# One decoder step: the stage between attention and the mLSTM state (output projection, norm, xm tiles, gates) put into one stated order

## The chip, the cores and the metric

The kernel runs on one core of one Trainium2 chip. A core has five engines with queues of their own: TensorE (PE, matrix products), VectorE (DVE), ScalarE (ACT), GpSimd (POOL) and SyncE (SP, which here issues most DMA transfers). Each engine takes its instructions in order; where one needs what another engine or a transfer makes, it waits on a semaphore, and everything behind it in the queue waits too. The metric is the device time of one execution in microseconds, as the median of several runs.

## What is computed

One inference step of a two-layer decoder with d_model 1024, for a prompt of 512 new tokens and 8 sample sequences with one new token each, so 520 token columns. Layer 0 is native sparse attention, layer 1 an mLSTM with four heads of width 512. All data are float32. The stage in question covers the end of layer 0 and the front of layer 1:

```python
x = x + out0 @ w_out0                      # layer 0: output projection and residual
h = rmsnorm(x, norm_w[1])
proj = h @ w_in                            # layer 1, 1024 -> 4096: xm and z
xm, z = proj[..., :D_INNER], proj[..., D_INNER:]
xpad = jnp.concatenate([conv_buf, xm], axis=1)
conv = conv_b
for j in range(CONV_W):                    # CONV_W = 4
    conv = conv + xpad[:, j:j + T] * conv_w[j]
c = jax.nn.silu(conv)
q = jnp.einsum('btnj,nji->btni', cb, w_qkv[0])     # blocks of 4 columns; cb = c, xb = xm in blocks
k = jnp.einsum('btnj,nji->btni', cb, w_qkv[1])
v = jnp.einsum('btnj,nji->btni', xb, w_qkv[2])
gpre = jnp.concatenate([q, k, v], axis=-1) @ w_gate + b_gate
ig, fl = gpre[..., :M_HEADS], jax.nn.log_sigmoid(gpre[..., M_HEADS:])
# then the mLSTM cell with states C, n, m; out = (hn * norm_w + skip * c) * silu(z); out @ w_out
```

## The kernel before

The activations lie transposed, features on the 128 partitions and the 520 tokens along the row, in two column halves of 260; the sample columns are the last 8 of half 1. A float32 product is made of three products of a reduced type: value and weight are each split into a high half (hi, a copy that rounds) and a low half (lo, the rest), and `mm3` issues hi x hi, lo x hi and hi x lo. In the trace a high or low half of a weight is called whi or wlo, of the normed input hhi or hlo, of the attention's result uo.

Weights come tile by tile (1024 x 128). `load_w` issues the transfer of the raw tile (wraw, 512 KB) on SP, the cast to whi on ACT, and the subtraction that gives wlo on DVE or POOL, by a table with a letter for each tile (LO_O for the output projection, LO_XM for xm). There are two buffers each of wraw, whi and wlo, so that a tile's parts overwrite those of the tile before the last.

The stage has these parts, in the order of the program:

- Output projection: a loop over 8 row tiles ft and the two halves c. For each, PE makes 24 matmuls into a PSUM buffer (mm), DVE adds the result to x1 (the residual stream, loaded from in_xT, called x in the trace), and `split_x` makes hhi on ACT and hlo on DVE. `rms_acc` squares x (ACT, sq) and adds it to a running sum sacc (DVE); `rms_close` sums it over the partitions with one PE product (s<-sacc) and makes the factor rr.
- `prepare`, spread between these: the gate weights folded with the block-diagonal q, k and v weights into FG (three wg products on POOL, three reduces ft on DVE), and the conv state's rows scv.
- xm loop over 16 tiles of layer 1's first projection: `xm_proj` for both halves (24 matmuls and one DVE eviction each), the next tile's `load_w`, three block-diagonal weights bd (POOL), `xm_tile` (causal conv, cva: one ACT and four DVE instructions), `xm_silu` (three on ACT, cvs, and the product CT on DVE), `xm_val` for the tile before (four matmuls t<-bd,xm and four copies to VT), `xm_gate` for the tile before that (products d for the sample columns, and, for each pair of tiles, eight matmuls s<-CT,FG and s<-xm,FG that add into the gate sums).
- Tail: the first z tile (`zm_tile(0)`), gates of tiles 14 and 15, `gate_samples` (a chain of some 15 small instructions on DVE and ACT from the sample columns of the gate sums, ss, to the decays sr, with two small PE products t<-ss and t<-sr), and the values of tile 15.

Then comes the state stage, where 64 state tiles cs of 512 KB are loaded, scaled, updated and stored.

What sets the order: the attention stage ahead and the state stage behind are recorded as pieces (one engine call, or one chain of matmuls into one buffer) and replayed in an order written as a table of numbers; all five engines then keep that order. Between the two, the order is of three kinds. In the output projection SP keeps the written order and the tile scheduler places the others. In the xm loop PE, ACT and DVE keep the written order; SP and POOL are placed. In the tail all are placed, with hints (`issue_after`). Every engine call goes through one helper, `Engine.call`, so that all instructions have its line, L407 before; groups are told apart by tile names.

Of the kernel before, what the change touches and what calls it, by code (L numbers as in the profile page):

```python
# [9 lines left out]
F32 = mybir.dt.float32  # L10
# [220 lines left out]
)  # L231
KSC = float(np.float32(512.0 ** -0.5))
# [97 lines left out]
class Pool:  # L330

    def __init__(self, rec, pool, bufs):
        self.rec, self.pool, self.bufs = rec, pool, bufs
# [7 lines left out]
class Rec:  # L341
# [8 lines left out]
    def cut(self):  # L350
        self.open = None

# [90 lines left out]
def step_kernel(ctx, tc, ap):  # L443
# [1054 lines left out]
    dctx.close()  # L1498
    r1 = ctx.enter_context(ExitStack())
# [16 lines left out]
    for k in range(4):  # L1516
        S.dma_start(x1[:, 2 * k:2 * k + 2], ap["xT"][:, 2 * k:2 * k + 2])
    def prepare():

        par0 = xp_.tile([128, 16, 7], F32, name="par0")  # L1520
        SP.dma_start(par0, ap["m_par"])
        wc0 = xp_.tile([128, 3, 16, 4], F32, name="wc0")
# [22 lines left out]
    for ft, c in [(ft, c) for ft in range(8) for c in range(2)]:  # L1545
        if ft not in wo:
            wo[ft] = load_w(ap["w_o"][ft], 8, eng=E[LO_O[ft]])
        if ft == 4 and c == 0:
            next(prep)
        w = wo[ft]  # L1550
# [4 lines left out]
        add = V.tensor_add(x1[:, ft, cs], x1[:, ft, cs], po[:, :CH])  # L1555
        if (ft, c) == (6, 0):
            with tc.issue_after(add.ins):
                next(prep, None)
        split_x(c, ft, x1[:, ft, cs], 1)
        if c:  # L1560
            S.dma_start(x1d[:, ft], x1[:, ft])
        rms_acc(sacc[c], ft == 0, x1[:, ft, cs], xn)
        if ft == 7:
            rms_close(c, sacc[c], xn)
    wx0 = load_w(ap["m_in"][0], 8, eng=E[LO_XM[0]])
    l0.close()
    xctx.close()
# [3 lines left out]
    l1 = ctx.enter_context(ExitStack())  # L1571
    cv = pool_of(l1, name="cv", bufs=1)
# [7 lines left out]
    l1s = pool_of(l1, name="l1s", bufs=1)  # L1580
# [32 lines left out]
    se = pool_of(l1, name="st0", bufs=1)  # L1613
# [18 lines left out]
    mctx = l1.enter_context(ExitStack())  # L1632
    mi = pool_of(mctx, name="mi", bufs=2)
    m1 = pool_of(mctx, name="mi1", bufs=1)
# [12 lines left out]
    def xm_proj(ft, c):  # L1647
# [5 lines left out]
        return V.tensor_mul(xm[:, c * CH:(c + 1) * CH], po[:, :CH], rr[c])  # L1653
# [3 lines left out]
    def xm_tile(ft):  # L1657
# [3 lines left out]
        S.activation(a, xm, AF.Identity, scale=par[:, ft, 3:4], bias=par[:, ft, 4:5])  # L1661
        for d in (1, 2, 3):
            V.scalar_tensor_tensor(a[:, d:512], xm[:, 0:512 - d], par[:, ft, 3 - d:4 - d], a[:, d:512],
# [4 lines left out]
    def xm_silu(ft):  # L1668
# [4 lines left out]
        G.tensor_scalar(CS[:, ft], ct[:, 512:520], par[:, ft, 6:7], None, op0=OP.mult)  # L1673
# [57 lines left out]
    def gates_of(gs, gi, gf, src):  # L1731
        V.tensor_copy(gs, src)
        for k, (nm, dst) in enumerate((("sel_i", gi), ("sel_f", gf))):
            po = xb()[:, :gs.shape[-1]]
# [3 lines left out]
    def gate_samples():  # L1738
        ss = m1.tile([128, 8, 8], F32, name="ss")
        gs, gi, gf, e, y, m0, m = (ss[:, k] for k in range(7))  # L1740
        gates_of(gs, gi, gf, pgt[1][:, CH - 8:CH])
# [15 lines left out]
    def gate_rows():  # L1757
        rows = [big(f"rows{i}", n=T) for i in range(3)]
        A_, W_, EM = rows
        gs = big("gs")  # L1760
        gi = big("gi")
        gf = big("gf")
        for c in range(2):
            cs = slice(c * CH, min((c + 1) * CH, T))
            gates_of(gs[:, cs], gi[:, cs], gf[:, cs], pgt[c][:, :min(CH, T - c * CH)])
        e = big("lse")
        y = big("lsy")
        log_sigmoid(*(x[:, :T] for x in (y, gf, e, gs)))

        V.memset(gs[:, 0:512], 1.0)  # L1770
        bcum = gf[:, 0:512]
        V.tensor_tensor_scan(bcum, gs[:, 0:512], y[:, 0:512], 0.0, op0=OP.mult, op1=OP.add)
        a = e[:, 0:512]
        V.tensor_sub(a, gi[:, 0:512], bcum)
        V.tensor_tensor_scan(A_, gs[:, 0:512], a, -HUGE, op0=OP.mult, op1=OP.max)
        m = gs[:, 0:512]
        V.tensor_add(m, bcum, A_)
        SP.dma_start(ap["o_mp"], m[:, 511:512])
        S.activation(EM, m, AF.Exp, scale=-1.0)
# [15 lines left out]
    for ft in range(16):  # L1795
        xst[ft] = [block_diag(mi, wc[:, t, ft], "bd", 12) for t in range(3)]
        xm_proj(ft, 0)
        if ft < 15:
            xm_load(ft + 1)
# [919 lines left out]
```

## Time and profile before

| | us |
|---|---|
| median of 3 runs (lowest, highest) | 1136.6 (1132.46, 1137.16) |
| the profiled execution | 1135.48 |
| its span, first to last instruction | 1132.8 |
| PE busy in the span | 1058.4 (93%) |
| DVE busy | 813.6 (72%) |
| ACT busy | 602.0 (53%) |
| POOL busy | 277.2 (24%) |
| the stage, first projection matmul to first matmul of z tile 1 | 210.74 |

The 2.7 us between span and execution lie outside the recorded instructions. Busy time is the union of an engine's instructions; matmuls overlap in the pipeline, so one takes 0.28 us in the record but the next may start 0.12 us after it. The clock column of a view is the share of full speed that was granted to PE in that stretch.

### The profile page before, as it was taken

Reading aid. Unit: us, or ns where it says so; the run is one execution under the profiler, and the core shown is the slowest. Engines: PE = TensorE matmul, PEld = TensorE weight load, DVE = VectorE, ACT = ScalarE, POOL = GpSimd, SP = SyncE. Lnnn points to the kernel's source line nnn. Section 1 sums busy time; section 2 is a strip of 40 time slices with the busy share of each in tenths; the row PEclk is TensorE's granted clock in tenths of the full one; section 3 lists DMA queues with packets and bytes.
Section 4 is the critical chain, followed back from the end, with each engine's and each line's share of the span. In section 5 each row is a group of like instructions: output and inputs, shape, how many; then the busy total and the mean of one; then the engine's idle time right before and its main releaser. Section 6 shows DMA issues by size and latency. Waiting matters only on the chain.

```text
span 1132.8 us, 24065 instructions
## 1 busy us (share of the span) xinstructions
PE 1058.4 (93%) x8563; PEld 929.7 (82%) x8563; DVE 813.6 (72%) x1988; ACT 602.0 (53%) x1326; POOL 277.2 (24%) x306
## 2 busy tenths in 40 slices
PE   6999999999998999999999998999999999999985
PEld 5999998999977867779888996798856577877885
DVE  7867744786489888857776676775666858878786
ACT  5332434545477766753444453666656746555544
POOL 3024233223201001004522231320222314232111
PEclk9999999999999899999999998999999999999988
DMA  7554643133436313455434451687698787969432
GB/s 231 166 189 132 204 126 117 38 101 119 137 97 208 94 57 118 143 192 163 134 132 135 166 168 65 221 268 277 194 310 304 233 277 236 364 198 317 167 82 88
DMA packets 124929, 197.18 MB, mean 174 GB/s; under 512 B 16253, under 2 KB 66302, under 8 KB 124554
## 3 DMA queue, kind: packets, MB, share of 16 engines
q1 hardware_dynamic: 116602, 181.32, 49.2%
q10 hardware_dynamic: 8208, 14.34, 3.5%
q8 instruction: 67, 1.10, 0.4%
q14 instruction: 52, 0.43, 0.1%
HBM read 145.89 MB, written 58.10 MB: 180 GB/s over the span
## 4 chain that ended last, share of the span: by engine, by line
PE 28%; DMA 10%; DVE 9%; issue 3%; ACT 3%; POOL 1%; SPq 1%; DVEq 0%; ACTq 0%; POOLq 0%
PE mm L407 18%; PE t L407 4%; PE s L407 4%; DMA zd<-zt 4%; DMA wraw<-in_m_in 4%; PE d L407 2%; ACT whi L407 1%; DVE x L407 1%; DMA wraw<-in_m_out 1%; DVE VT L407 1%; DVE sacc L407 1%; DVE zt L407 1%; SPq L407 1%; DVE wlo L407 1%; DVE CT L407 1%
## 5 line engine op out<-in xcount | busy, mean ns | idle before, releaser
L407 PE MATMUL mm<-hhi,whi 128*128 128x260 f32 (+1 forms) x976 | 283.2, 290 | 10.4 <-DVE zt L407 6.7
L407 PE MATMUL mm<-hhi,wlo 128*128 128x260 f32 (+1 forms) x976 | 278.5, 285 | 5.3 <-DVE wlo L407 5.3
L407 PE MATMUL mm<-hlo,whi 128*128 128x260 f32 (+1 forms) x976 | 277.2, 284 | 0.0
L407 PEld LDWEIGHTS mm<-hhi,whi 128*128 128x128 f32 (+1 forms) x976 | 183.9, 188 | 19.6 <-issue 7.7
L407 PEld LDWEIGHTS mm<-hhi,wlo 128*128 128x128 f32 (+1 forms) x976 | 183.9, 188 | 7.0 <-DVE wlo L407 6.7
L407 PEld LDWEIGHTS mm<-hlo,whi 128*128 128x128 f32 (+1 forms) x976 | 183.7, 188 | 0.7
L407 POOL TENSOR_TENSOR wlo<-wraw,whi 128x1024 fp32r<-128x1024 f32 (+1 forms) x52 | 106.6, 2051 | 255.7 <-ACT whi L407 239.0
L407 ACT ACTIVATE whi<-wraw 128x1024 fp32r<-128x1024 f32 (+1 forms) x98 | 88.9, 908 | 115.6 <-PE mm L407 53.2
L407 DVE SCALAR_TENSOR_TENSOR cs<-t,wk,cs 128x512 f32<-128x512 f32 x128 | 88.4, 743 | 14.0 <-PE t L407 9.9
L407 ACT ACTIVATE s<-s,mn 128x512 f32<-128x512 f32 (+3 forms) x128 | 71.3, 559 | 27.3 <-DVE mn L407 25.4
L407 ACT ACTIVATE cs<-cs,SBC 128x1024 f32<-128x1024 f32 x64 | 70.7, 1141 | 15.0 <-PE d L407 15.0
L407 PE MATMUL s<-phi,w1h 128*128 128x256 f32 (+1 forms) x256 | 77.9, 304 | 0.7 <-DVE hs L407 0.5
L407 PE MATMUL s<-plo,w1h 128*128 128x256 f32 (+1 forms) x256 | 74.8, 292 | 2.5 <-DVE plo L407 2.5
L407 DVE TENSOR_TENSOR wlo<-wraw,whi 128x1024 fp32r<-128x1024 f32 (+2 forms) x50 | 54.6, 1093 | 30.7 <-ACT whi L407 30.3
L407 PE MATMUL s<-phi,w1l 128*128 128x256 f32 (+1 forms) x256 | 74.7, 292 | 0.0
L407 PE MATMUL mm<-uh,whi 128*128 128x260 f32 x224 | 66.9, 299 | 2.8 <-ACT sq L407 2.8
L407 DVE CUSTOM_DVE_ANT_0 s<-s,D 128x512 f32<-128x512 f32 (+3 forms) x128 | 59.4, 485 | 9.7 <-PE s L407 8.6
L407 PE MATMUL mm<-uh,wlo 128*128 128x260 f32 x224 | 64.3, 287 | 0.0
L407 PE MATMUL mm<-ul,whi 128*128 128x260 f32 x224 | 64.2, 287 | 0.0
L407 PEld LDWEIGHTS s<-plo,w1h 128*128 128x128 f32 x256 | 49.2, 192 | 3.2 <-POOL wlo L407 2.2
L407 PE MATMUL s<-KA,qst 128*128 128x256 f32 (+3 forms) x128 | 48.5, 385 | 2.3 <-DVE mn L407 1.6
L407 PEld LDWEIGHTS s<-phi,w1h 128*128 128x128 f32 x256 | 49.0, 192 | 1.5 <-PE mm L407 0.7
(425 smaller groups left out, 2605.1 us busy)
## 6 DMA issues: line engine op xcount, KB each, us to landing
cs<-in_state_C SPq DMA_DIRECT2D x64, 512.0 KB, 5.4
o_cs<-cs SPq DMA_DIRECT2D x64, 512.0 KB, 4.9
praw<-in_cache SPq DMA_DIRECT2D x128, 128.0 KB, 2.4
dk<-in_cache SPq DMA_DIRECT2D x128, 128.0 KB, 2.2
wraw<-in_m_in SPq DMA_DIRECT2D x32, 512.0 KB, 4.2
wraw<-in_m_out SPq DMA_DIRECT2D x32, 256.0 KB, 3.8
wraw<-in_w_kv SPq DMA_DIRECT2D x11, 512.0 KB, 4.8
wraw<-in_w_q SPq DMA_DIRECT2D x8, 512.0 KB, 3.3
```

The source lines that it names most:

```text
L407: return f(*[real(x) for x in a], **{n: real(x) for n, x in k.items()})
```

## The change

Everything from the output projection through the values of tile 15 is recorded as well, 712 pieces, and replayed with `R.run(NE, CALLS1, MOVED1)`, with the order of all five engines as in the table CALLS1. MOVED1 lists 97 pieces that go to another engine (`swapped`): eight casts to whi from ACT to DVE (output tiles 3 and 5, xm tiles 0, 1, 5, 7, 8, 9); 28 of the 64 VT copies from DVE to ACT; five CT products and ten of the 14 sacc adds from DVE to POOL; seven wlo from DVE to POOL (output tiles 2, 3, xm tiles 4, 5, 6, 7, 9) and five from POOL to DVE (output tiles 4 to 7, xm tile 0); 25 of the 48 bd products, the three wg and three scv products, one FG sum, wkr and one z product from POOL to DVE. The loads of x1 and the stores of it (x1d) go from ACT's queue to SP's. par0 and wc0 move to a pool that stays open through the xm loop, which reads them in place of par and wc. The pools of layer 0 are closed and those of layer 1 opened by two recorded pieces on SP (`to_layer_1`, `to_xm`) in the middle of the stage. `gate_rows`, which nothing calls, is deleted.

```diff
+CALLS1 = (
+    21, 0, 66, 44, 28, 64, 70, 65, 63, 15, 22, 1, 3, 26, 2, 4, 16, 25, 29, 45, 46, 108, 9, 5, 6, 30, 8, 60, 17,
...
+MOVED1 = (
+    20, 30, 36, 43, 45, 46, 52, 62, 67, 68, 69, 71, 72, 73, 86, 88, 89, 95, 102, 105, 112, 117, 124, 127, 147,
...
     def __init__(self, rec, pool, bufs):
-        self.rec, self.pool, self.bufs = rec, pool, bufs
+        self.rec, self.pool, self.bufs, self.barrier = rec, pool, bufs, None
...
+    def later(self, fn, tiles, pools):
+
+        for p in pools:
+            p.barrier = len(self.pieces)
+        self.fn("SP", 0.0, 0.0, fn, w=tiles)
...
+    R.on = True
+    for k in range(8):
+        uo[k] = R.have(uo[k], [128, 2, NTOK], F32R)
...
     for k in range(4):
-        S.dma_start(x1[:, 2 * k:2 * k + 2], ap["xT"][:, 2 * k:2 * k + 2])
+        SP.dma_start(x1[:, 2 * k:2 * k + 2], ap["xT"][:, 2 * k:2 * k + 2])
+    par0 = pr_.tile([128, 16, 7], F32, name="par0")
+    wc0 = pr_.tile([128, 3, 16, 4], F32, name="wc0")
...
         if c:
-            S.dma_start(x1d[:, ft], x1[:, ft])
+            SP.dma_start(x1d[:, ft], x1[:, ft])
...
+    def to_layer_1():
+        l0.close()
+        ctx.enter_context(l1)
+        cv.pool, l1s.pool = (pool_of(l1, name=n, bufs=1).pool for n in ("cv", "l1s"))
...
+    R.later(to_layer_1, list(uo.values()), (cv, l1s))
+    R.later(to_xm, list(uo.values()) + [xp_, xn], (se, mi, m1))
...
-    order_ = ctx.enter_context(ExitStack())
-    order_.enter_context(tc.manual_schedule(engines={mybir.EngineType.PE, mybir.EngineType.Activation,
-                                                   mybir.EngineType.DVE}))
     for ft in range(16):
-        xst[ft] = [block_diag(mi, wc[:, t, ft], "bd", 12) for t in range(3)]
+        R.at("xmw", ft)
+        xst[ft] = [block_diag(mi, wc0[:, t, ft], "bd", 12) for t in range(3)]
...
         if ft < 13:
-            with tc.issue_after(last["w"]):
-                win_copy(ft)
-                if ft in (3, 6, 9):
-                    win_copy(12 + ft // 3)
+            for n in [ft] + ([12 + ft // 3] if ft in (3, 6, 9) else []):
+                R.fn("SP", 0.4, 1.0, lambda n=n: win_copy(n), r=[xms[ft + 1][0][0]])
...
     xm_silu(15)
-    order_.close()
...
     xm_val(15)
+    with tc.manual_schedule(engines=every):
+        R.run(NE, CALLS1, MOVED1)
     mctx.close()
     pctx.close()
```

In the projection the order of PE's row tiles and halves was (0,0), (0,1), (1,0), (1,1) and so on; now it is (1,1), (1,0), (0,0), (0,1), (3,1), (3,0), (2,0), (2,1), (4,1), (4,0), (5,1), (5,0), (6,0), (6,1), (7,0), (7,1), then the first sum s<-sacc, xm tile 0's half 0, and the second sum.

DVE at the start of the projection. The x rows are adds of a matmul result to x1; sacc and hlo are as above. Before:

```order
L407 TENSOR_TENSOR uo<-us,uo 128x8 x8
L407 TENSOR_TENSOR x_9218<-x_9218,mm 128x260 x3
L407 SCALAR_TENSOR_TENSOR hlo_9195<-x_9218,nw,hhi_9193 128x260
L407 SCALAR_TENSOR_TENSOR hlo_9196<-x_9218,nw,hhi_9194 128x260
L407 SCALAR_TENSOR_TENSOR hlo_9195<-x_9218,nw,hhi_9193 128x260
L407 TENSOR_TENSOR sacc_9223<-sacc_9223,sq 128x260
L407 TENSOR_TENSOR x_9218<-x_9218,mm 128x260
L407 TENSOR_TENSOR wlo<-wraw,whi 128x1024 x2
```

and now:

```order
L461 TENSOR_TENSOR uo<-us,uo 128x8 x8
L461 TENSOR_TENSOR x_9238<-x_9238,mm 128x260 x2
L461 CAST whi<-wraw 128x1024
L461 TENSOR_TENSOR x_9238<-x_9238,mm 128x260 x2
L461 SCALAR_TENSOR_TENSOR hlo_9380<-x_9238,nw,hhi_9345 128x260
L461 TENSOR_TENSOR wg<-wg,wc_9246 128x512
L461 SCALAR_TENSOR_TENSOR hlo_9391<-x_9238,nw,hhi_9383 128x260
```

The cast is that of output tile 3; it stands between the adds of tile 1 and those of tile 0, and its subtraction is now on POOL, while two subtractions that stood on DVE further down are gone.

PE at the end of the stage. d<-CT,bd and d<-xm,bd are a tile's gate products, s<- its gate sums, mm<-hhi the first z tile, t<-ss and t<-sr the two sample products, t<-bd,xm the values of tile 15, t<-cst,VS and t<-gs the start of the state stage. Before:

```order
L407 MATMUL s<-CT_9834,FG 32x260
L407 MATMUL s<-xm_11278,FG 32x260
L407 MATMUL d<-CT_9834,bd 128x8 x2
L407 MATMUL d<-xm_11278,bd 128x8
L407 MATMUL t<-ss,cst 128x8 x2
L407 MATMUL t<-sr,cst 128x24 x4
L407 MATMUL t<-bd,xm_11278 128x128 x4
L407 MATMUL t<-cst,VS 8x128 x4
```

and now (the second half of z tile 0, 24 matmuls, is left out at the dots):

```order
L461 MATMUL t<-ss,cst 128x8 x2
L461 MATMUL d<-CT_11200,bd 128x8 x2
L461 MATMUL d<-xm_11084,bd 128x8
L461 MATMUL s<-CT_11002,FG 32x260
L461 MATMUL s<-xm_10814,FG 32x260
L461 MATMUL s<-CT_11090,FG 32x260
L461 MATMUL s<-xm_10825,FG 32x260
...
L461 MATMUL d<-CT_11090,bd 128x8 x2
L461 MATMUL d<-xm_10825,bd 128x8
L461 MATMUL t<-sr,cst 128x24 x4
L461 MATMUL t<-bd,xm_11298 128x128 x4
```

Between t<-ss and t<-sr, where before stood nothing, now stand the products of tiles 13 and 11, half of a gate sum and half of z tile 0; behind the values of tile 15 come more gate sums, which before stood ahead.

SP where the projection ends. wraw<-in_m_in is the load of an xm tile, o_conv a store of xm tile 0. Before:

```order
L407 DMA stm<-in_state_m 128x8
L407 DMA wraw<-in_m_in 128x1024
L407 DMA o_conv<-xm_9901 128x11
L407 DMA o_vwin<-in_vwin 16x8176
```

with two loads of xm tiles further up, and now:

```order
L461 DMA x1d<-x_9238 128x520
L461 DMA nT<-in_state_n 128x128
L461 DMA par<-in_m_par 128x112
L461 DMA o_vwin<-in_vwin 16x8176
L461 DMA wraw<-in_m_in 128x1024
L461 DMA stm<-in_state_m 128x8
L461 DMA o_conv<-xm_9883 128x11
```

with three further up: the load of the fourth xm tile now stands ahead of the first o_conv store, where before it was the third's.

## Rows read from the trace of the kernel before

**Rows 1.** The busy time of each engine in five stretches that make up the stage: the projection, the xm loop up to its last matmul, the first z tile, the sample gates and values, and the start of the state stage. Columns: stretch, its length, then busy us and instructions of PE, PE's weight loads, DVE, ACT and POOL, the granted clock, the DMA share and GB/s.

```profile
499.70:553.55 53.85, 48.49 (x388) 47.00 (x387) 36.25 (x62) 20.58 (x47) 19.51 (x14) 1.00 0.50 167
553.55:685.84 132.29, 125.95 (x1088) 119.53 (x1086) 94.14 (x218) 58.57 (x83) 40.87 (x67) 1.00 0.42 141
685.84:691.70 5.86, 5.86 (x53) 5.86 (x50) 3.54 (x10) 2.71 (x6) 0.31 (x1) 1.00 0.03 5
691.70:704.60 12.90, 8.13 (x54) 6.25 (x52) 6.85 (x39) 4.00 (x11) 1.34 (x3) 0.77 0.13 32
704.60:710.44 5.84, 5.82 (x23) 1.98 (x24) 3.79 (x16) 2.61 (x4) 0.00 (x0) 0.63 1.02 402
sum 210.74, PE 194.25 PEld 180.62 DVE 144.57 ACT 88.46 POOL 62.02; mean PE 38.85 PEld 36.12 DVE 28.91 ACT 17.69 POOL 12.40
```

**Rows 2.** What PE waited for, from the views of its waits: the first three rows in the projection (499.7 to 553.55), the next two in the xm loop (553.55 to 686), the last two in the tail. Columns: total us, times, longest.

```profile
PE mm L407 <- DVE x L407: 2.6, 3, 1.5
PE s L407 <- DVE sacc L407: 2.0, 1, 2.0
PE mm L407 <- DVE wlo L407: 0.6, 1, 0.6
...
PE mm L407 <- DVE wlo L407: 5.3, 7, 0.9
PE mm L407 <- ACT whi L407: 1.0, 1, 1.0
...
PE t L407 <- DVE sr L407: 3.5, 1, 3.5
...
PE t L407 <- DVE gs L407: 1.3, 1, 1.3
```

**Rows 3.** The view of waits of all engines in the stage, the row of ACT's casts.

```profile
ACT whi L407 <- DMA wraw<-in_m_in: 42.5, 12, 4.8
```

**Rows 4.** The timeline at the start of the stage: a row of PE, then of ACT, DVE and ACT's queue. Columns: start, length, engine and operation, and in brackets the idle time before it and what ended it.

```profile
507.17 0.51 PE L407 MATMUL mm<-uo,whi 128*128 128x260 f32 x2 [1.54 <-DVE x L407]
...
501.01 0.89 ACT L407 ACTIVATE uo<-us 128x8 fp32r<-128x8 f32 x8
...
501.75 0.70 DVE L407 TENSOR_TENSOR uo<-us,uo 128x8 fp32r<-128x8 f32 x8
...
502.60 1.79 ACTq L407 DMA_DIRECT2D x<-in_xT  x4
```

**Rows 5.** The timeline of PE in the tail.

```profile
692.36 0.41 PE L407 MATMUL s<-CT,FG 128*32 128x260 f32 x1
...
693.91 0.61 PE L407 MATMUL d<-CT,bd 128*128 128x8 f32 x4
...
694.60 0.59 PE L407 MATMUL t<-ss,cst 128*128 128x8 f32 x4
698.71 0.62 PE L407 MATMUL t<-sr,cst 128*128 128x24 f32 x2 [3.52 <-DVE sr L407]
```

**Rows 6.** Windows of the tail, PE alone: stretch, length, PE busy and instructions, granted clock, DMA share and GB/s.

```profile
696.00:698.00 2.00, 0.00 (x0) 1.00 0.33 131
698.00:708.00 10.00, 8.02 (x31) 0.53 0.45 150
708.00:710.00 2.00, 2.00 (x14) 0.78 1.05 407
710.00:712.00 2.00, 2.00 (x17) 1.00 0.59 177
```

**Rows 7.** The groups of instructions by form: of DVE and POOL in the stage, and, the two CAST rows, of DVE in the whole span. Columns: names, shapes, count, busy us, mean ns of one, idle time before them.

```profile
L407 DVE TENSOR_TENSOR wlo<-wraw,whi 128x1024 fp32r<-128x1024 f32 x17 | 21.5, 1270 | 22.3 <-ACT whi L407 22.3
L407 DVE SCALAR_TENSOR_TENSOR hlo<-x,nw,hhi 128x260 fp32r<-128x260 f32 x16 | 17.2, 1084 | 6.3 <-ACT hhi L407 6.3
L407 DVE COPY VT<-t 128x128 f32<-128x128 f32 x64 | 14.0, 279 | 1.6 <-PE t L407 1.6
...
L407 DVE TENSOR_TENSOR CT<-cva,cvs 128x520 f32<-128x520 f32 x16 | 11.5, 720 | 3.4 <-ACT cvs L407 3.4
L407 DVE TENSOR_TENSOR sacc<-sacc,sq 128x260 f32<-128x260 f32 x14 | 7.5, 539 | 0.0
...
L407 POOL TENSOR_TENSOR bd<-cst,wc 128x128 f32<-128x128 f32 x48 | 30.4, 662 | 69.9 <-PE d L407 62.7 <-DVE rr L407 7.2
L407 POOL TENSOR_TENSOR wlo<-wraw,whi 128x1024 fp32r<-128x1024 f32 x6 | 14.6, 2429 | 30.2 <-ACT whi L407 30.2
...
L407 DVE CAST phi<-praw 128x1024 fp32r<-128x1024 f32 x20 | 16.5, 835 | 14.3 <-PE s L407 8.4 <-ACT hsg L407 5.3 <-ACT plo L407 0.4
...
L407 DVE CAST whi<-wraw 128x1024 fp32r<-128x1024 f32 x3 | 2.0, 682 | 0.0
```

**Rows 8.** A POOL subtraction and a DVE instruction that overlap, from the timelines of the two, and from the view by tile the shortest, median and longest hlo in ns.

```profile
521.53 2.39 POOL L407 TENSOR_TENSOR wlo<-wraw,whi 128x1024 fp32r<-128x1024 f32 x1 [18.01 <-ACT whi L407]
521.89 2.32 DVE L407 SCALAR_TENSOR_TENSOR hlo<-x,nw,hhi 128x260 fp32r<-128x260 f32 x1 [1.00 <-ACT hhi L407]
...
L407 DVE SCALAR_TENSOR_TENSOR hlo<-x,nw,hhi x16: 483/489/2579, 510.7 to 555.5; 128x260 fp32r<-128x260 f32 x16
```

**Rows 9.** The windows view, columns as in rows 1, of two stretches with a stated order: projections in the attention layer, and the start of the state stage.

```profile
40.00:120.00 80.00, 79.52 (x619) 78.97 (x619) 56.65 (x95) 28.15 (x82) 21.76 (x18) 0.98 0.56 175
720.00:740.00 20.00, 18.03 (x134) 15.88 (x133) 16.73 (x25) 13.13 (x23) 6.43 (x7) 0.91 0.55 191
```

More of the change, by code (lines that the diff above doesn't have):

```diff
@@ L351, in cut, with have @@
         self.open = None
+    def have(self, tile, shape, dtype):
+        b = Base(None, shape, dtype, {})
+        b.t = tile
+        return Lazy(b)
+    def later(self, fn, tiles, pools):
+        for p in pools:
+            p.barrier = len(self.pieces)
+        self.fn("SP", 0.0, 0.0, fn, w=tiles)
     def add(self, eng, m, a, k):
@@ L1498, in step_kernel @@
     dctx.close()
+    R.on = True
+    for k in range(8):
+        uo[k] = R.have(uo[k], [128, 2, NTOK], F32R)
+    for k in wo:
+        wo[k] = [R.have(t, [128, 8, 128], F32R) for t in wo[k]]
     r1 = ctx.enter_context(ExitStack())
@@ L1755, in gate_samples @@
         V.tensor_copy(SBC.rearrange("p h a b -> p (h a b)"), po[:, 0:96])
[L1757 to L1779, printed above, removed]
-        V.tensor_scalar(EM, EM, XMAX, None, op0=OP.min)
-        na = se.tile([128, 1], F32, name="na")
-        V.tensor_scalar(na, A_[:, 511:512], -1.0, None, op0=OP.mult)
-        S.activation(W_, a, AF.Exp, bias=na)
-        V.tensor_scalar(W_, W_, KSC, None, op0=OP.mult)
-        po = xb()
-        for i in range(4):
-            PE.transpose(po[:, i * 128:(i + 1) * 128], a[:, i * 128:(i + 1) * 128], ident)
-        V.tensor_copy(aT, po.rearrange("p (i h r) -> p i h r", i=4, h=4)[:, :, :, 0])
-        for i in range(3):
-            SP.dma_start(rd[:, i], rows[i][0:128:32])
@@ L1807, in step_kernel @@
             xm_silu(ft - 1)
-        late = xm_proj(ft, 1)
+        R.at("xm", ft, 1)
+        xm_proj(ft, 1)
         if ft > 1:
+            R.at("gate", ft - 2)
             xm_gate(ft - 2)
+        R.at("conv", ft)
         conv[ft] = xm_tile(ft)
+        R.at("misc")
         if ft == 8:
@@ L1817, in step_kernel @@
             c_load(ft + ECS - 16)
+    R.at("silu", 15)
     xm_silu(15)
-    order_.close()
-    G.tensor_mul(wkr, wkr, wc[:, 0].unsqueeze(2).to_broadcast([128, 16, 4, 4]))
-    with tc.issue_after(late.ins):
-        V.tensor_reduce(mw, wkr, axis=AX.X, op=OP.add)
-        V.tensor_scalar(nwm, par[:, :, 5], -0.5, None, op0=OP.mult)
+    R.at("misc")
+    G.tensor_mul(wkr, wkr, wc0[:, 0].unsqueeze(2).to_broadcast([128, 16, 4, 4]))
+    V.tensor_reduce(mw, wkr, axis=AX.X, op=OP.add)
+    V.tensor_scalar(nwm, par[:, :, 5], -0.5, None, op0=OP.mult)
+    R.at("zm", 0)
     zm_tile(0)
+    R.at("gate", 14)
     xm_gate(14)
+    R.at("gate", 15)
     xm_gate(15)
+    R.at("gsamp")
     gate_samples()
+    R.at("val", 15)
     xm_val(15)
+    with tc.manual_schedule(engines=every):
+        R.run(NE, CALLS1, MOVED1)
     mctx.close()
```

52 lines of the change are left out of this document (31 added, 21 removed), and 36 rows, old and new, of tables (CALLS1, MOVED1).

## The prediction

> **What bounds the kernel now.** I read three views: the windows of the stage that the change touches, the waits of TensorE (PE) in it, and the timeline of its two ends. The stage runs from the first output-projection matmul to the first matmul of the second z tile, 210.74 us of the 1132.8 us span, and PE is busy for 194.25 of them [rows 1]: PE is the bound, and nothing else comes near it (VectorE, DVE, 144.57; ScalarE, ACT, 88.46; GpSimd, POOL, 62.02). So a change of order can win only what PE idles or does slowly. Idle is 5.36 us in the projection (53.85 − 48.49), 6.34 us in the xm loop (132.29 − 125.95) and 4.77 us in the tail (12.90 − 8.13) [rows 1]. The slow part follows from the last one: PE stands still from 696 to 698, its granted clock then reads 0.53 on the mean of the next ten microseconds (the lower of its two levels, 1.2 against 2.4 GHz, for nearly all of them), and it is back at 1.00 in the slice from 710 [rows 6]. The 8.02 us of busy PE at 0.53 would be about 4.0 to 4.3 at the upper level, and the 2.00 at 0.78 about 1.6: the clock costs some 4.3 us. All that there is to win is 16.5 + 4.3 = 20.8 us.
>
> The waits that hold the idle time [rows 2]: in the projection three for x (2.6), one for the sum of squares (DVE sacc, 2.0), one for the low half of a weight (DVE wlo, 0.6); in the xm loop seven more for low halves (5.3) and one for a high half (ACT whi, 1.0); in the tail one for the sample decays (DVE sr, 3.5), one for a gate row's copy (DVE gs, 1.3).
>
> **The change part by part.** All sums are made against the profiled execution, 1135.48 us with its span of 1132.8; the median of the three runs shown is 1136.6, 1.1 us above it. Outside the stage the order is the same, so I leave the rest of the span as it is.
>
> *Start of the stage: +2.2 us.* PE begins with column half 1, which contains the eight sample columns. Their high halves start at 501.01 on ACT and the low ones at 501.75 on DVE [rows 4]; the first of eight is through at about 501.9, where before PE began at 499.70 with half 0. 501.9 − 499.7 = 2.2.
>
> *x: −2.6 us.* The three waits for x go: with half 1 first, the add of half 0 comes two projection halves later (about 3 us each: 16 of them in 53.85 us with 5.36 idle), and it was only 1.54 us late [rows 4]; the two short ones are PE waiting for an add to free a PSUM buffer, and I count such waits once, below. The load of x goes from ACT's queue to SP's, but behind the same release of its pool at 502.6 [rows 4], so I take it to land as before. The weights of tiles 3 and 2 are now queued behind it; they have until 513.8 and later. The eight x1d stores, issued by SP instead of ACT, stand ahead of weight loads that wait for a buffer anyway: nothing.
>
> *A new wait at output tile 3: +3.2 us.* The cast of that weight goes from ACT to DVE and its subtraction from DVE to POOL. The cast writes the buffer that tile 0's high half holds, so it waits for PE's last matmul on tile 0, and PE's next piece is tile 3. Price: one DVE cast of 128x1024, between 0.682 us and 0.835 us [rows 7], and one POOL wlo of 2.429 us [rows 7], less nearly nothing that PE can do meanwhile: 3.1 to 3.3. Queued behind the waiting cast on DVE are the two adds of tile 0, then the hlo pieces, three wg products and three reduces; ACT's hhi pieces wait for these adds. I add **+1.0 us** for a second wait, at tile 2's other half, where an add stands behind this backlog and PE needs its PSUM buffer. Its bounds are 0 and the 2.39 us of one POOL wlo alongside [rows 8].
>
> *End of the projection: −2.6 us.* The wait for sacc (2.0) goes, because the sum for half 0 now stands behind tile 7's second half, and the one for half 1 behind the first xm half; ten of the 14 adds go to POOL. So does the wait for a low half (0.6), with two more of these sums off DVE there. Projection: 2.2 − 2.6 + 3.2 + 1.0 − 2.6 = **+1.2 us**: it gets no shorter.
>
> *xm loop: −4.3 us.* The loads are issued one tile earlier (before the first o_conv store SP now has four of them and before had three), and with a tile's two halves at about 6 us plus its val and gate pieces, that puts a landing of some 4 us and the two conversions well before PE's turn. So the remaining waits on weights (5.3 + 1.0 = 6.3) go. What comes back I take from a part of this kernel that has the same load and conversion chain under a stated order already, 40 to 120: 0.48 us idle in 80 [rows 9]; at the other end the state stage, 720 to 740, idles 1.97 in 20 [rows 9]. For 130 us that is 0.8 to 13; the loop is like the first (weight tiles and evictions, no large state loads), so near the low end: 2.0. −6.3 + 2.0 = −4.3.
>
> DVE's load doesn't decide it by its sum. It gains eight casts (8 x 0.68 to 0.84 = 5.5 to 6.7), 25 bd products (between a VT copy's 0.279 and POOL's 0.662: 7.0 to 16.6; a DVE instruction on 128 columns is nearer the first), and some 4 us of wg, scv and wkr; it gives away 28 VT copies to ACT (7.8), five CT (3.6) and ten sacc products (5.4) and, net, two wlo (2.5) [rows 7]. That is −3 to +8 on 144.57. ACT, busy for 88.46 of the 210.74 us, gives 8 casts and takes 28 copies of a similar sum. The deferred val and gate pieces change no PE work, only its place.
>
> *The tail: −8.1 us.* Between the small product of the sample gates (t<-ss, from 694.60) and that of the decays (t<-sr, from 698.71) stands a chain on DVE and ACT, and PE waits 3.52 us for its end with nothing else to do [rows 5]. Now PE has four pieces there: gate 13's and gate 11's products d, 0.69 each (693.91 to 694.60 [rows 5]); half of a gate sum, about 0.5 (all of it took from 692.36 to 693.91 with a wait of some 0.4 in it [rows 5]); and half of z tile 0, 24 matmuls, 2.9 (all of it fills the 5.86 us before 691.70 [rows 1]). 0.7 + 0.7 + 0.5 + 2.9 = 4.8 against 3.5, so the wait goes (−3.5). The gs wait goes with it, since DVE has its pieces of the tail earlier (−1.3). Without the 2 us of nothing, the clock has no reason in this trace to fall, so −4.3. Against this stands +1.0: PE meets the first state product earlier, and its load (three cs issued early now, others after the sample work) can be the next thing late. −3.5 − 1.3 − 4.3 + 1.0 = −8.1. The cover has 1.3 us in hand; what DVE does for other pieces within the chain (the evictions of z tile 0) can take that, and then PE stands still for part of a microsecond, not for 3.5.
>
> *Pools, par0/wc0, deleted gate_rows: nothing.* They change which buffer is read, and when its pool opens; PE's next piece doesn't wait on either.
>
> **Sum:** +1.2 − 4.3 − 8.1 = −11.2; 1135.5 − 11.2 = **1124 us** (1124.3).
>
> **The rivals.**
>
> *DVE and POOL block each other (1133 us).* One hlo that met a POOL wlo of 2.39 us took 2.32, where the median of the 16 is 0.489 [rows 8] and their mean 1.084 [rows 7]. The excess is 16 x (1.084 − 0.489) = 9.5 us, with six wlo on POOL. After there are eight wlo there, plus ten sacc and five CT products; if the same 9.5 lands between PE's evictions in the xm loop, the loop gives nothing and loses some 5: 1124 + 9 = 1133, no change to speak of. Against it: POOL's sum falls by 25 bd products (16.6 us), and PSUM has more than one buffer in hand. The Trainium skill, "SBUF — State Buffer", Reading the diagram under "SBUF: two separate sides", has this as a rule: the port pair that the two share is an exclusive lock for a whole instruction, so the loser fully blocks. The trace agrees (2.32 beside 2.39); by that rule it is not POOL's sum but its long instructions that count, and those grow from six to eight.
>
> *The casts on DVE wait for their loads (1145 us, slower).* ACT waited 42.5 us in 12 waits for weight loads in this stage, 3.5 on the mean and 4.8 at most [rows 3], and nobody cared: ACT has the slack. Six of the eight moved casts belong to xm tiles (0, 1, 5, 7, 8, 9). The load's landing is what the cast waits for. If loads are still that late, DVE stands still with evictions and conv rows behind it, and PE waits for these: 6 x 3.5 = 21 us, 1124 + 21 = 1145. It decides from the point where a load is issued less than a landing (about 4 us) ahead of DVE's turn. Against it: the load is a tile earlier than before, if one of the two raw buffers is free by then.
>
> *Everything is covered (1118 us).* The +3.2 and +1.0 of the projection overlap the slack, the xm loop keeps 0.8 and not 2: 1124.3 − 4.2 − 1.2, and −1.0 if the first state load is in time too, gives 1118. The floor, with all 20.8 us won, is 1135.5 − 20.8 = 1114.7.
>
> *The change doesn't do what it says (1135 us).* The compiler's order could have the pieces elsewhere; but the built program has them in the stated order, so this has little weight.
>
> **How the numbers follow.** Forecast (1120 to 1130) 0.54; blocked DVE (1130 to 1138) 0.19; casts that wait (1138 to 1150) 0.10; all covered (1114 to 1120) 0.15; not done 0.02. A measurement tells about 0.5% from no change, 5.7 us, so faster means below 1131. Faster: 0.54 + 0.15 + a small part of the blocked case, 0.02 = 0.71; slower (above 1142): 0.09; the same: 0.20. The range leaves out most of the slower rival and the top of the blocked one: 1114 to 1135, where also the bounds of the xm loop (0.8 to 13 idle) lie.
>
> **What would show it.** Right: PE idle for some 3 us at output tile 3 with POOL's wlo as releaser; no slice with PE at 0.00 and no clock at 0.50 before the second z tile; the wlo waits below 3 us in all; the stage near 199 us. Wrong: PE waiting for x or xm evictions in the loop with DVE over 90% busy there; DVE waiting for wraw loads; or the half clock again, moved behind a wait for the first state load.

## The result, and the profile after

The changed kernel took 1121.81 us (median of 4 runs, 1120.31 to 1123.59) against 1136.21 for the kernel before (4 runs, 1132.46 to 1137.16): a ratio of 0.988, 95% interval 0.9851 to 0.9909, so 1.2% faster. Its profiled execution took 1123.16 us with a span of 1121.2, 11.6 below the span of before.

The stage, now from PE's last attention instruction (501.24; the projection starts 1.6 us later, which did not happen before) to the first matmul of z tile 1, in the windows view, to be laid beside [rows 1]:

```profile
501.24:555.81 54.57, 50.13 (x386) 49.52 (x386) 34.99 (x65) 18.02 (x43) 14.50 (x13) 0.94 0.52 174
555.81:676.50 120.69, 120.69 (x1046) 116.25 (x1045) 94.41 (x211) 60.56 (x103) 43.46 (x53) 1.00 0.49 159
676.50:694.70 18.20, 17.22 (x149) 14.52 (x145) 9.25 (x50) 5.82 (x19) 1.10 (x3) 0.91 0.05 17
694.70:698.72 4.02, 4.02 (x23) 1.38 (x24) 3.57 (x16) 2.43 (x3) 0.00 (x0) 1.00 1.01 368
sum 197.48, PE 192.06 PEld 181.66 DVE 142.23 ACT 86.83 POOL 59.06; mean PE 48.02 PEld 45.42 DVE 35.56 ACT 21.71 POOL 14.76
```

The stage fell from 210.74 to 197.48 us, by 13.3: 11.1 of it are PE's idle time (16.5 before, 5.4 now) and 2.2 its busy time (194.25 and 192.06). The stage begins 1.5 us later in this execution (501.24 against 499.70), which is the difference to the span's 11.6; everything behind it takes 422.4 and 422.5 us (1132.8 − 710.44 and 1121.2 − 698.72). That this last part agrees so well is chance: no edit of this document touches its order, and over all traces here it takes 418.6 to 426.7 us. Row 2 is the reading that matters: from the projection's end to the first z tile PE is busy for 120.69 of 120.69 us. What PE still waits for in the stage, against [rows 2]:

```profile
PE mm L461 <- POOL wlo L461: 1.6, 1, 1.6
PE mm L461 <- ACT uo L461: 1.6, 1, 1.6
PE mm L461 <- DVE x L461: 1.0, 1, 1.0
PE t L461 <- DVE gs L461: 1.0, 1, 1.0
PE mm L461 <- DVE uo L461: 0.2, 1, 0.2
```

Of the old waits only the one for gs is left. New are the wait for the sample columns (uo, two rows) at the start and two at output tile 3: one named x, for an add that has to empty a PSUM buffer, and one for wlo. The second is the foreseen one; in the timelines of PE, DVE and POOL:

```profile
517.61 0.50 PE L461 MATMUL mm<-uo,whi 128*128 128x260 f32 x2 [1.00 <-DVE x L461]
519.71 0.39 PE L461 MATMUL mm<-uo,wlo 128*128 128x260 f32 x1 [1.60 <-POOL wlo L461]
...
516.53 0.69 DVE L461 CAST whi<-wraw 128x1024 fp32r<-128x1024 f32 x1 [5.24 <-DMA x<-in_xT]
517.14 0.75 DVE L461 TENSOR_TENSOR x<-x,mm 128x260 f32<-128x260 f32 x2
...
517.30 4.86 POOL L461 TENSOR_TENSOR wlo<-wraw,whi 128x1024 fp32r<-128x1024 f32 x2 [12.50 <-DVE whi L461]
```

DVE's cast starts at 516.53, when tile 0's buffer comes free. The adds stand behind it, so PE waits for a PSUM buffer until 517.61; then it issues two matmuls and waits for POOL's subtraction, which began at 517.30. (The row names a load as what ended DVE's 5.24 us of idleness. PE's timeline points to the buffer: its last two matmuls with tile 0's high half start at 516.09 and take 0.40.)

What no term foresaw is in the windows of the clock, to be laid beside [rows 6]:

```profile
502.00:504.00 2.00, 0.92 (x3) 0.81 0.00 0
504.00:506.00 2.00, 2.00 (x11) 0.50 0.61 102
506.00:508.00 2.00, 2.00 (x17) 0.83 0.97 386
520.00:522.00 2.00, 2.00 (x13) 0.58 0.75 150
522.00:524.00 2.00, 2.00 (x12) 0.57 1.03 320
684.00:686.00 2.00, 2.00 (x15) 0.54 0.00 0
686.00:688.00 2.00, 2.00 (x13) 0.61 0.07 10
```

Three short stretches at the lower level have taken the place of the long one: behind the wait at the start, behind the one at tile 3, and in the tail at 684, where PE had not waited at all but had worked on small products since 679.5. The clock missing from their rows, 2 us x (1 − clock) summed, is 1.7 us each, 5.1 in all; by the same sum the long stretch of before comes to 5.1. Over PE's busy time alone the clock cost about 4.2 us before and 4.9 now. So in this execution the clock gave nothing back, and the gain is in the waits.

### The profile page after: what moved, and what is told of

It is laid out like the page before. It is cut to its first block, busy times and chain, and to the rows that moved or that the text cites. A ratio compares the mean times of both kernels' runs of the same rounds, so it can differ in the third digit from the quotient of the medians.

```text
span 1121.2 us, 24010 instructions
## 1 busy us (share of the span) xinstructions
PE 1058.3 (94%) x8563; PEld 931.7 (83%) x8563; DVE 812.1 (72%) x1985; ACT 600.8 (54%) x1346; POOL 274.3 (24%) x289
## 5 line engine op out<-in xcount | busy, mean ns | idle before, releaser
L461 POOL TENSOR_TENSOR wlo<-wraw,whi 128x1024 fp32r<-128x1024 f32 (+1 forms) x54 | 111.9, 2073 | 243.5 <-ACT whi L461 208.7
L461 ACT ACTIVATE whi<-wraw 128x1024 fp32r<-128x1024 f32 (+1 forms) x90 | 80.5, 894 | 82.4 <-PE mm L461 63.2
L461 DVE TENSOR_TENSOR wlo<-wraw,whi 128x1024 fp32r<-128x1024 f32 (+2 forms) x48 | 52.2, 1088 | 9.6 <-ACT whi L461 9.0
L461 PE MATMUL mm<-uo,whi 128*128 128x260 f32 x256 | 49.7, 295 | 2.8 <-ACT uo L461 1.6
```

The lines of the kernel that those rows point to most:

```text
L461: return f(*[real(x) for x in a], **{n: real(x) for n, x in k.items()})
```

## The experiments

Every edit is to the replay call alone (`exchange` swaps pieces' places in the order, `behind` puts pieces directly behind another). Since the times of versions so close overlap, the stage of each trace is the measure, from PE's last attention instruction to the first matmul of z tile 1 (from the first projection matmul where that comes first). "Idle" is its length less PE's busy time, "clock" the sum of 2 us x (1 − clock) over its two-microsecond windows. The kernel before, run again beside the others, had medians of 1134.43 us (10 runs, beside e1 to e4), 1132.96 (20, e5 to e8), 1133.01 (12, e9 and e10) and 1128.8 (3, e11 and e12).

| run | stage | idle | clock | median us (runs) |
|---|---|---|---|---|
| before | 210.7 | 16.5 | 5.1 | 1136.21 (4) |
| changed | 197.5 | 5.4 | 5.1 | 1121.81 (4) |
| e9_same, the changed kernel again | 195.5 | 6.1 | 1.7 | 1119.26 (6) |
| e1_half0_first | 195.9 | 5.3 | 3.4 | 1116.36 (4) |
| e2_tile2_first | 193.8 | 4.7 | 1.7 | 1116.08 (4) |
| e3_z_ahead | 198.7 | 6.9 | 5.1 | 1123.06 (7) |
| e4_z_sooner | 196.1 | 5.4 | 3.4 | 1120.09 (4) |
| e5_no_moves | 198.2 | 7.3 | 3.4 | 1125.09 (8) |
| e6_casts_act | 196.9 | 5.9 | 3.4 | 1121.08 (2) |
| e7_loads_late | 198.0 | 6.6 | 3.4 | 1123.64 (5) |
| e8_together | 195.9 | 4.2 | 5.1 | 1117.23 (6) |
| e10_small_in_a_row | 198.6 | 8.6 | 1.7 | 1122.53 (3) |
| e11_as_late_as_before | 252.8 | 41.1 | | 1172.36 (2) |
| e12_late_on_act | 250.5 | 40.7 | | 1173.9 (2) |

**The changed kernel again.**

> The changed kernel once more, unaltered, for a second profile of it and more times. The traces so far show the granted clock at 0.50 behind the wait for the sample columns in some runs and not in others, with the same wait (1.6 and 0.25 us), and in the tail likewise. Theory: whether the clock falls there depends on where in time the stretch falls, not on the program, so that this run can lack one or both of the stretches that the first profile had (504 to 507 and 684 to 687), and then its stage is 194 to 196 instead of 197.5, with the same waits of PE to 0.1 us. Rival: it is a matter of the program: both stretches are there again, stage 197.0 to 198.0.

```profile
502.00:504.00 2.00, 2.00 (x13) 0.60 0.48 85
504.00:506.00 2.00, 2.00 (x12) 0.55 0.98 371
520.00:522.00 2.00, 2.00 (x19) 1.00 1.06 324
522.00:524.00 2.00, 2.00 (x18) 1.00 0.62 213
...
684.00:686.00 2.00, 2.00 (x20) 1.00 0.04 2
```

These windows of the second profile have the stretch at the start and neither of the others; all waits came back, and a second short one for x (0.7 us) beside them. So two profiles of one program differ by 2 us in the stage, mostly by the clock. The theory holds for the stage and the clock, and for the waits but for that 0.7. This sets the scale for every run below: a stage that differs by 2 us says nothing unless idle time or a named wait goes with it.

**Half 0 first.**

```diff
+    order = exchange(CALLS1, (21, 15), (22, 16))
```

> Output tile 1's two halves trade places, so PE begins with half 0, which needs no sample columns. The stage (from PE's last attention instruction to the first matmul of z tile 1) takes 197.5 us in the changed kernel, of which 1.85 us are PE's wait for the sample columns at its start, and some 1.6 us are lost because the granted clock reads 0.50 in the 2 us behind that wait. Theory: wait and half clock belong together and both go; the add of half 0 then waits for x (landed at about 508), which costs 1.3 us: stage 197.5 - 1.85 - 1.6 + 1.3 = 195.4. Rival: the half clock comes from the small products at the end of attention, whatever the wait: stage 197.0. Second rival: the wait for x takes the clock down in its turn: 197 to 198.

The wait for the sample columns is gone and no low clock followed the start, but PE then waited 1.73 us for x, so idle time moved by 0.1. Behind this wait the clock stayed at 1.00; it fell in the window from 514, at the waits for tile 3. The gain in the stage is the clock's, and of that the run before shows that it varies by itself. By waits alone the column half with which PE begins makes no difference: late sample columns and late x cost the same.

**Tile 2 ahead of tile 3.**

```diff
+    order = exchange(CALLS1, (53, 31), (47, 37), (54, 32), (48, 38), (55, 33),
+                     (56, 34), (49, 39), (50, 40), (57, 41), (46, 30))
```

> Output tiles 2 and 3 trade places on all engines; loads and casts stay where they are. Tile 2's high half goes into a buffer that is free after tile 1, tile 3's into the one that tile 0 holds until PE's last matmul on it. Theory: the two waits at tile 3 (1.60 for POOL's low half, 1.00 for an add behind DVE's cast) are the price of that buffer, and with tile 2's 6 us of matmuls between they go: stage 197.5 - 2.6 = 194.9, no wait of PE on a POOL low half. Rival: the wait only moves, since the add still stands behind the cast on DVE and POOL makes both low halves one behind the other: stage 196.5 to 197.5.

PE's waits in the stage:

```profile
PE mm L475 <- DVE x L475: 1.9, 3, 1.1
PE mm L475 <- ACT uo L475: 1.6, 1, 1.6
PE t L475 <- DVE gs L475: 1.0, 1, 1.0
PE mm L475 <- DVE uo L475: 0.3, 1, 0.3
```

The wait for POOL's low half is gone: it was the price of the shared buffer. But the wait for an add stays (1.1, since the adds still stand behind the cast) and two short ones come (0.4 each), so idle time fell by 0.7 and not 2.6. Theory and rival each had half. The stage of 193.8 is below both, because the clock cost 3.4 us less than in the first profile.

**The second z half ahead, and sooner.**

```diff
+    order = behind(CALLS1, 659, 665)                    # e3
...
+    order = behind(CALLS1, 684, 665, 636, 580)          # e4
+    order = behind(order, 704, 637, 638)
```

> The second half of z tile 0 goes back to where it stood before the change, directly behind the first, so that only 1.9 us of PE work are left between the two sample products. Theory: that half is the cover of the chain from ss to sr (3.5 us in the kernel before), so PE waits 1.6 us for sr, and the clock falls behind the wait for some 3 us: stage 197.5 + 1.6 + about 1.5 = 200.6, minus up to 1.5 if the dip at 684 (0.54 to 0.61 over 4 us) was this half's alone: 199.1 to 200.6. Rival: the chain is shorter now, since DVE has less of other work around it, and nothing is lost: stage 197.5 or less.

> The second half of z tile 0 goes to directly behind the product t<-ss, ahead of gate 13's d and half a gate sum, which now follow it; the copies of gate 13's d go behind the sample chain on DVE. In the changed kernel PE was busy from 679.5 to 684.2 with small products only and never waited, and yet the granted clock read 0.54 and 0.61 from 684 to 688, which cost that half about 1.5 us (4.49 against 2.98). Theory: the dip comes from the long row of small products; cut from 4.7 to 3.3 us it does not come, or comes shorter: stage 196.0 to 197.0. Rival: it comes all the same behind any such row, or the next row of small products (now longer) has it: 197.5 to 198.

PE's wait in e3 and its clock behind it:

```profile
PE t L475 <- DVE sr L475: 1.5, 1, 1.5
...
682.00:684.00 2.00, 2.00 (x20) 0.92 0.00 0
684.00:686.00 2.00, 0.47 (x3) 0.50 0.07 10
686.00:688.00 2.00, 2.00 (x10) 0.50 0.00 0
688.00:690.00 2.00, 2.00 (x15) 0.50 0.00 0
690.00:692.00 2.00, 2.00 (x21) 0.88 0.33 131
```

With the cover taken away, the wait for sr is back with 1.53 us against 1.6 expected, and a stretch at the lower level over some 7 us with it, twice what the tail had in the changed kernel. That z half is what hides the sample chain. The stage of 198.7 is just below the 199.1 to 200.6 expected. Against what was expected, the clock did not fall behind the wait: the wait begins at 684.06, and the window before it, with PE busy throughout, already reads 0.92. In e4 idle time is the changed kernel's (5.43 against 5.42) and the tail stretch is missing, as expected; but it is missing in e9 too, so e4 shows only that nothing is lost by it.

**No engine moves; casts back on ACT.**

```diff
-        R.run(NE, CALLS1, MOVED1)
+        R.run(NE, CALLS1, ())                                          # e5
...
+    casts = (45, 88, 156, 173, 280, 342, 373, 405)
+        R.run(NE, CALLS1, [n for n in MOVED1 if n not in casts])       # e6
```

> The order of the pieces stays, but no piece changes its engine (MOVED1 empty): the casts go back to ACT, 28 VT copies, five CT and ten sacc products to DVE, and so on. Theory: the order does most of the work, and DVE's sum, busy 94 of 121 us in the xm loop, grows by about 5 us net (VT 7.8, CT 3.6, wlo 5.5, less bd 25 x 0.41 and casts 6 x 0.73): it stays below PE's, so PE waits a few microseconds: stage (197.5, of which 1.7 us are the tail's half clock and 1.7 that of the start, either of which can be absent) 199 to 202. Rival: the order was fitted to the moves and falls apart without them: stage over 205, with waits for evictions (DVE xm, x) all through the loop.

> Only the eight casts go back from DVE to ACT, in the same places of the order; all else as changed. Theory: no cast in the xm loop waits for its load any more, ACT is busy 61 of 121 us there, so either engine does: stage 197.5, within 1 us apart from the half-clock stretches, and no wait of PE in the loop. Rival: ACT's 1.06 us against 0.73, and its place behind the conv chain, bring waits for whi or wlo back: stage 199 or more. Second rival: DVE was what lengthened the wait at output tile 3, and the stage gets 1 us shorter.

PE's longest waits in e5, beside the one for the sample columns:

```profile
PE mm L475 <- DVE x L475: 2.7, 1, 2.7
PE s L475 <- DVE sacc L475: 1.8, 1, 1.8
```

Without any of the 97 moves idle time is 7.3 us, 1.2 to 1.9 more than with them, all of it in the projection (one wait of 2.71 for x, one of 1.83 for sacc); the xm loop again has none. With only the casts back on ACT it is 5.9, within what two profiles of the changed kernel differ by. So in the stage's idle time the moves are worth at most 2 of the 11 us. The times leave room for more: 1125.09 us is 0.9922 of the kernel before (0.9894 to 0.9949), beside 0.9885 (0.9846 to 0.9924) for the changed kernel in e9, and these intervals overlap. Against the expectation, DVE's load did not grow in e5: it is busy for 141.4 us of the stage, and for 142.2 in the changed kernel. SP's queue for x1, par0 and wc0 and the pools are as changed in every one of these versions, so what these are worth apart from the order is not shown.

**Loads one place later, and two.**

```diff
+    order = CALLS1                                                     # e7
+    for load, store in ((216, 178), (246, 205), (279, 235), (309, 268), (341, 298), (372, 330), (404, 361),
+                        (437, 393), (470, 423), (500, 459), (532, 489), (562, 521), (594, 551)):
+        order = behind(order, store, load)
...
+    for load, store in ((216, 205), (246, 235), (279, 268), (309, 298), (341, 330), (372, 361), (404, 393),
+                        (437, 423), (470, 459), (500, 489), (532, 521), (562, 551), (594, 582)):
+        order = behind(order, store, load, load + 1, load + 2)         # e11; e12 with the casts of e6
```

> Each load of xm tiles 3 to 15 goes one place back on SP: behind the o_conv store of tile k-3, where it now stands behind that of tile k-4 (and before the change behind that of tile k-2). Theory: the early loads are what took away the 6.3 us of waits for weights in the loop; with about 8 us less of lead, five of the casts on DVE wait for their loads by up to some 4 us each, evictions queue behind them, and PE waits again: stage up by 3 to 8 us, with DVE or ACT waiting for wraw<-in_m_in. Rival: the lead was more than needed and the order of the conversions did it: no wait of PE in the loop, stage as it was.

> Load, cast and low half of xm tiles 3 to 15 all go to behind the o_conv store of tile k-2, which is where the load stood before the change; the casts of tiles 5, 7, 8 and 9 stay on DVE. One place later had cost 1.2 us of idle time, with no wait for a weight (run with the loads one place back). Theory: the lead of the loads is what removed the 6.3 us of waits, and two places are where it runs out: waits of PE for whi or wlo at most tiles again, 6 us and more, and, where DVE makes the cast, DVE idle for the load by 3 to 5 us at four tiles (tiles 0 and 1 are not moved) with evictions behind it: stage 197.5 + 6 to + 20. Rival: the lead was never needed, the order of the rest is: idle time within 2 us of the changed kernel's 5.4 to 6.1.

> As the run before, with loads, casts and low halves as late as before the change, and the eight casts on ACT instead of DVE. Theory: ACT then waits for the loads as it did before the change (42.5 us in 12 waits), DVE doesn't, and PE's waits for weights come back at some 0.5 to 1 us a tile for 13 tiles: stage 197.5 + 6 to + 13, and below the run before. Rival: which engine waits makes no difference, since the low half follows the cast anyhow: both runs within 1.5 us of each other in PE's idle time.

One place later, idle time was 1.2 us above the first profile of the changed kernel and 0.6 above the second, and no wait for a weight came back: the rival holds, there is that much lead to spare. It is about all the lead there is. Before the change ACT's casts waited 42.5 us for loads [rows 3]. In the changed kernel no cast of the loop waits for its load; ACT's casts wait for PE to free a buffer (first row). In e7 three wait for loads again (the other two):

```profile
ACT whi L461 <- PE mm L461: 6.7, 5, 3.3
...
ACT whi L475 <- DMA wraw<-in_m_in: 4.2, 2, 3.1
...
DVE whi L475 <- DMA wraw<-in_m_in: 0.4, 1, 0.4
```

Two places, with cast and subtraction moved to directly behind the load, cost 51 us by the medians. PE's longest waits in e11, and what DVE and ACT waited for:

```profile
PE d L475 <- DVE QKS L475: 11.4, 3, 5.2
PE mm L475 <- DVE xm L475: 6.4, 4, 3.0
PE d L475 <- DVE CT L475: 5.4, 2, 4.4
PE d L475 <- DVE VS L475: 4.7, 2, 4.3
PE mm L475 <- POOL wlo L475: 4.6, 3, 1.6
...
ACT whi L475 <- DMA wraw<-in_m_in: 48.0, 9, 7.3
DVE wlo L475 <- ACT whi L475: 34.0, 7, 7.3
...
DVE whi L475 <- DMA wraw<-in_m_in: 17.1, 4, 4.8
...
595.10 0.69 DVE L475 CAST whi<-wraw 128x1024 fp32r<-128x1024 f32 x1 [3.88 <-DMA wraw<-in_m_in]
595.71 0.48 DVE L475 COPY VT<-t 128x128 f32<-128x128 f32 x2
...
596.14 2.05 PE L475 MATMUL t<-bd,xm 128*128 128x128 f32 x8 [4.55 <-DVE VT L475]
```

PE hardly waits for weights (4.6 us). It waits for small copies and evictions of earlier tiles, which stand on DVE behind a subtraction or a cast that waits for a load (the last three rows: a cast waits 3.88 us, two VT copies stand behind it, and PE waits 4.55 us for them). DVE's 51 us of waiting for casts and loads stand beside 41 us of idle PE, 36 more than in the changed kernel, and the clock, 0.89 to 0.90 over these stages, takes most of the rest. Before the change the load stood in the same place on SP and cost PE 6.3 us, with DVE waiting 22.3 us for whi [rows 7]. So the 51 us are not the price of the load's place alone. The conversions moved too, and loads two places later with the conversions left in their places were not tried. It makes no difference which engine casts (252.8 and 250.5, idle 41.1 and 40.7), since the subtraction follows the cast and is on DVE for most tiles.

**One row of small products.**

```diff
+    order = behind(CALLS1, 622, 659)
```

> The first half of z tile 0 goes ahead, directly behind xm tile 15's last half, so that values, gate sums and sample products, which it parted into 7 and 4.7 us, now stand in one row of some 11.7 us; nothing else moves and PE's work is the same. Theory: the clock falls in long rows of small products although PE is busy all the time: a stretch at 0.50 begins within that row, and the stage is 1.5 to 4 us longer than the changed kernel's without its tail stretch (195.8), so 197.3 to 200. Rival: only standing idle takes the clock down: clock at 1.00 through the row, stage 195 to 196.

The longest wait in the row, and the windows in it and behind it:

```profile
PE t L475 <- ACT VT L475: 1.6, 1, 1.6
...
678.00:680.00 2.00, 0.37 (x9) 1.00 0.00 0
680.00:682.00 2.00, 2.00 (x20) 1.00 0.02 4
```

The clock stayed at 1.00 through the row, even behind a wait of 1.6 us in it, while idle time grew by 2.5 to 3.2 us, most of it from waits that the new place brought. Theory and rival both fail here: neither the row nor standing idle lowered the clock. The stage of 198.6 lies in the theory's range by luck, since waits and not the clock put it there.

**All three edits.**

```diff
+    order = exchange(CALLS1, (21, 15), (22, 16), (53, 31), (47, 37), (54, 32), (48, 38), (55, 33),
+                     (56, 34), (49, 39), (50, 40), (57, 41), (46, 30))
+    order = behind(order, 684, 665, 636, 580)
+    order = behind(order, 704, 637, 638)
```

> Three earlier edits in one: half 0 of output tile 1 first, output tile 2 ahead of tile 3, the second half of z tile 0 directly behind t<-ss. By the idle time of their traces: PE waits 1.73 us for x instead of 1.85 for the sample columns, 1.0 to 1.9 instead of 2.6 at tiles 2 and 3, 1.0 at gs. Theory: these add up, and both half-clock stretches stay away because neither a wait nor a long row of small products is left: stage 191.5 to 192.5 (197.5 less 0.1, 1.0, 1.7 and 1.7, less some for x), span some 5 us below that of the changed kernel, so about 1116 by the median. Rival: the half clock shifts to another place, as it did in the run with tile 2 first (0.52 to 0.62 from 686 to 690, behind the wait for gs): stage 193.5 to 194.5.

The rival's mechanism came, beyond its range of 193.5 to 194.5: idle time is the least of all, 4.15 us, but the clock's windows from 684 to 696 read 0.74, 0.50, 0.50, 0.50, 0.50, 0.70 and took back what the waits had given. The median is 1117.23 (6 runs, 1114.89 to 1122.74; ratio to before 0.987, 0.9838 to 0.9903) beside 1119.26 (1113.75 to 1127.11) for the changed kernel in its second set: not told apart.

## Why the prediction held, step by step

It gave 1124 us, 11.2 below the profiled execution; measured are 12.3 by the profiled executions and 14.4 by the medians. The path was right: PE bounds the stage, and of the waits that the order was to remove all but the one for gs went. That the total came so close is in part luck. Of the forecast 11.2 us, 6.9 were idle time and 4.3 the clock; in the first profile they are 11.1 of idle time, 2.2 of busy time and nothing from the clock. The waits gave 4.2 us more than forecast and the clock 4.3 less, and the two errors cancel. The second profile of the same kernel is another 6.4 us shorter (1116.75 us). One of the signs that the prediction set for being right failed with the clock term: there is a granted clock of 0.50 in the stage again. The terms:

- *Start, +2.2.* 1.59 + 0.25 = 1.84 us of waiting. What was not in the sum is the clock behind it.
- *x, −2.6.* Right for the long wait, and e1 shows it from the other side: with half 0 first it is back with 1.73.
- *Tile 3, +3.2, and tile 2, +1.0.* Right in place and releaser, too large in size: 1.00 + 1.60 in place of 3.2. The chain of cast and subtraction took the 3.2 that I gave it (516.53 to 519.71), but PE had the end of tile 0 and two matmuls to do in it. The backlog showed only in the second profile (0.7). e2 shows that the buffer was the cause of 1.6 of it; the add behind the cast, of the rest.
- *End of the projection, −2.6.* Right: no wait for sacc or a low half is left. The projection, 54.57 against 53.85, is 0.7 longer against 1.2 forecast, with two low-clock stretches in it.
- *xm loop, −6.3 + 2.0.* The first half is right, the second was 2.0 too much: no idle time at all in 120 us. The bound that I took it from (40 to 120, 0.48 us in 80 [rows 9]) was the better guide, and I rounded it up. My words for the cause were too narrow as well. I put it on loads that are issued earlier by one tile; they stand two places earlier, behind the store of tile k−4 and not k−2, and e7 shows that one of these is spare. That the casts' waits for loads are gone is seen in the traces; how much of the 6.3 us is the loads' lead and how much the order of the rest is not shown, since no run has the one without the other. e11 shows what a late load can do in a stated order: it stops whatever stands behind its conversions.
- *Tail, −8.1.* sr (−3.5) right, and shown by e3. gs (−1.3) wrong: 0.98 remain. The last gate sum is through at about 693.2, but its copy stands on DVE behind eight small products (pr, wk, nT) and starts at 694.13. The clock's −4.3 was the term that failed: over the stage it came to nothing in the first profile and to 3.4 us in the second. I gave the stretch of before one cause, the idle time ahead of it, and 1.7 us of low clock came in the tail without any wait in one profile and not in the other; the other 3.4 us of the first profile stand behind the new waits in the projection, which my sum gave no clock. The first state load (+1.0) was in time.

The terms that were off had both signs: tile 3, the loop and the state load cost less, clock and gs more.

The rivals: DVE and POOL did not block each other more than before. The mean hlo fell from 1.084 us [rows 7] to 0.577, though POOL's subtractions went from six to eight; fewer of them met an hlo. In the projection, where the hlo pieces are, POOL made five subtractions before, and five hlo took 1.62 to 2.58 us; now it makes two there, and one hlo took 1.81. Other pieces took some of it (the 128x8 add to cva went from 0.188 to 0.414). The casts that wait for their loads were the right danger: with loads and conversions both late, e11 and e12 cost 51 to 52 us more and not 21, on either engine. By e7 the order keeps clear of it by one place. What stays open is when the clock falls: behind 1.84 us of waiting at the start it did in nine of the eleven traces that have this wait (not in e2 and e3), in the tail with and without a wait ahead of it, and in e10 not at all in the tail. These runs do not settle it.

## What to carry to other kernels

When PE is 93% busy, count its idle time and its half-speed time in the stage that a change touches: their sum is the most that can be won, and here a stated order won two thirds of it. In a stated order, look at how far a load and its conversions stand ahead of their first use before you look at which engine converts: here the engine made no difference with early loads (e6) or late ones (e12). One place of the load's lead was spare. Loads two places late with their conversions directly behind them cost 51 us, because unrelated small work queued behind the conversions. Before small gains are weighed by medians, take two profiles of one program: here they differed by 2 us in the stage, with 3.4 us of clock between them. And check a sum term by term: this one came out right with two errors of 4 us in it that cancelled.

## What was not expected of the hardware

The granted clock fell with PE busy throughout (0.54 and 0.61 from 684 to 688 in the first profile), and in the second profile of the same program it stayed at 1.00 behind the same work. Each of the short stretches in the first profile cost 1.7 us of clock. The Trainium skill, "TensorE: Matmul & The Clock Gate", What's actually happening under Part 1, says that the watch on activity behind the gate is not reset when a kernel starts, and that the number of matmuls which one kernel runs at the lower level differs from run to run for this reason. The two profiles of the changed kernel agree that it differs (5.1 and 1.7 us of clock); the reason no run here shows.
